# Conditioning units turned feature-major on VectorE, sums folded, a root spread by one product, and a 128-row spatial product for the samples

## The chip, the cores and the metric

The kernel runs on one core of a Trainium2 chip. The core has five engines with a queue each: TensorE (PE in the profile; its weight loads are PEld), VectorE (DVE), ScalarE (ACT), GpSimd (POOL) and SyncE (SP, which here issues nearly all transfers). Matrix products write to PSUM, a small memory of eight banks of 128 rows by 512 fp32 numbers; everything else lies in SBUF, 128 rows ("partitions") wide. The metric is the device time of one execution in microseconds, taken as the median of several runs. Less is better.

## What is computed

One step of a one-layer decoder for 256 prompt tokens and 8 samples of 4 tokens each: 288 tokens of 2048 features, all in fp32. Nine conditioning vectors (one of the prompt, eight of the samples) give six modulation vectors of 2048 features each.

```python
def _rms(x, gain):
    y = xf * lax.rsqrt(jnp.mean(xf * xf, axis=-1, keepdims=True) + EPS)
    return (y * gain.astype(jnp.float32)).astype(x.dtype)
...
    mod = (jax.nn.silu(c) @ w_ada + b_ada).reshape(n, N_MOD, 1, D_MODEL)
    sh_m, sc_m, gt_m, sh_f, sc_f, gt_f = [mod[:, i] for i in range(N_MOD)]

    h = _rms(x, g_mix) * (1 + sc_m) + sh_m
    proj = h @ w_in
    ...
    z = c_gate * hc
    ...
    ya = b_gate * conv

    u = jax.nn.gelu(u)
    v = _rms(jax.nn.gelu(v), g_v)
    vg = v.reshape(n, s // chunk, chunk, SG_GROUPS, SG_HEAD)
    w_causal = jnp.tril(w_sg[:, :chunk, :chunk])
    sp = jnp.einsum('gts,bnsgc->bntgc', w_causal, vg) + b_sg[:, :chunk].T[None, None, :, :, None]
    yb = u * sp.reshape(n, s, SG_DIM)

    merged = jax.nn.sigmoid(ga) * (ya @ w_pa) + jax.nn.sigmoid(gb) * (yb @ w_pb)
    x = x + gt_m * (merged @ w_out)

    h2 = _rms(x, g_ffn) * (1 + sc_f) + sh_f
    gate, up = jnp.split(h2 @ w_ffn_in, 2, axis=-1)
    x = x + gt_f * ((jax.nn.silu(gate) * up) @ w_ffn_out)
```

The outputs are the normalised `x` of both groups, the last rows of the convolution's input, and the normalised `v` rows.

## The kernel before

**Layout.** Activations are feature-major: a tile holds 128 features in its rows and the 288 tokens in its columns (256 of the prompt, then 32 of the samples). The weights stream from HBM in blocks of 1 MB or less into seven `raw` buffers. ACT rounds a segment of up to four 128x128 tiles to fp32r (`hi`, L444) and DVE makes the rest of it (`lo`, L450); there are four buffers of each. The activations are split in the same way (`split`, L274). One weight tile times one activation tile is a *triple* of three products (`triple`, L217 to L226): hi by hi, hi by lo, lo by hi.

**Order.** PE's order is that of the program throughout. Until the step `free`, the order of ACT, DVE and SP is the program's too; after it a planner orders them by its own estimate of which instruction is ready. POOL is always the planner's. The list `steps` holds blocks of weights (`Blk.run`), conditioning blocks (`Ada.run`) and small steps (`Do`). Small work on PE between triples goes through `later(f, gap)`: `drain`, called after each triple, runs the first entry of the list `pending` when `gap` triples have passed since the entry before it.

**Conditioning units.** The 96 blocks of 128 modulation features come in eight units (`ADA_UNITS`, L36). A unit of the kind `ks == 1` (aE, a2, a3, a4, a5) covers 16 feature blocks. For each of the 16 blocks of the contraction, four products with 32 columns of conditioning vectors (nine used) as weights and 512 columns of `w_ada` as the moving side run side by side on the four column quarters of the array, and leave a condition-major result in the bank `ada`: quarter j, rows 32j to 32j+8, holds feature blocks 4j to 4j+3 of the unit. `Ada.tail` (L387) copies it to SBUF on ACT (L390); three triples later four fp32 products with a selection matrix `sel` as the moving side (L400) make it feature-major, and four DVE adds (L404) put it into `mod` with the bias `b_ada`. The units aA, aC and aD (`ks == 2`) add two halves on the way, with `selk`.

**Norms.** `SquareSum` keeps a sum of squares in `acc` and the last square apart in `last`. `token_rstd` (L168) makes the sums over features on PE: three products with a column of ones for `acc`, and three for `last` into the same PSUM columns (`sums`, `square_sum` at L185); each product covers 128 tokens, at offsets 0, 128 and 160. `roots` (L194) scales them on DVE, and POOL raises them to the power -1/2 (L199). `token_rstd` serves the norm of `v` (`v_stats`) and the second norm (`rstd2`). The first norm (`sums1`, from the step `root`) has one set of sums, and the last one (`finish`) calls `sums` itself. `rstd_bcast` (L203) spreads the roots over 128 rows for norm 1 (`norm1`), norm 2 (`norm2`) and the end, with three fp32 products (L208): a root column, repeated, as weights by an identity, 128, 128 and 32 tokens wide; the last of them uses 32 rows of the array.

**Spatial gating.** `v_transpose` turns `v` token-major (L761) and scales it by the root and `g_v` (L763). For the samples (`tb == 2`) only rows 96 to 127 are scaled, which are the 32 sample tokens. `sg_load` loads and masks the spatial weights. `spatial(g)` (L795) makes three fp32 products for each of eight groups: two chunks of the prompt (L801, L802; 128 rows) and the samples (L803; 32 rows, 32 columns wide).

Of the kernel before, what the change touches and what calls it, by code (L numbers as in the profile page):

```python
# [29 lines left out]
GC = 0.044715  # L30
EPS = 1e-6

C_BADA, C_GMIX, C_SEL, C_SELK, C_ID, C1_END = np.cumsum([0, 96, 16, 36, 18, 128]).tolist()
C_GFFN, C_GFIN, C_WCONV, C_STATE, C_MASK, C_MASKS, C2_END = np.cumsum([0, 16, 16, 24, 128, 128, 32]).tolist()

ADA_UNITS = [  # L36
# [52 lines left out]
def _body(tc, nc, d, pc, pw, pslot, ptmp, pps):  # L89
    ids = [0]  # L90

    def nm(s):
        ids[0] += 1
        return f"{s}_{ids[0]}"
# [4 lines left out]
    def slot(dt=F32, shape=(P, T)):  # L99
        return pslot.tile(list(shape), dt, tag="s", name=nm("s"), padded_shape=[P, TU])  # L100

    def tmp(n=T):
        return ptmp.tile([P, n], F32, tag="t", name=nm("t"), padded_shape=[P, TU])
# [4 lines left out]
    def psmisc():  # L108
        return pps.tile([P, 512], F32, tag="misc", name=nm("px"), bufs=3)
# [15 lines left out]
    ident = cp1[:, C_ID : C_ID + 128]  # L125
    mask = cp[:, C_MASK : C_MASK + 128]
    masks = cp[:, C_MASKS : C_MASKS + 32]
    sel = cp1[:, C_SEL : C_SEL + 36]
    selk = cp1[:, C_SELK : C_SELK + 18]

    x = const("x", [P, 16, T])
# [35 lines left out]

    def token_rstd(ss, n, half=False, gaps=None):  # L168
        got = {}
        steps = [lambda: sums(got, ss, True), lambda: sums(got, ss, False), lambda: roots(got, n, half)]  # L170
        for f, gap in zip(steps, gaps or (0, 0, 0)):
            if gaps:
                later(f, gap)
            else:
                f()
        return got

    def sums(got, ss, first):
        if first:
            got["ps"] = psmisc()  # L180
        square_sum(got["ps"], ss.acc if first else ss.last, first, not first)
# [12 lines left out]
    def roots(got, n, half):  # L194
        ps = got["ps"]
        r = got["r"] = ptmp.tile([P, 3], F32, tag="r", name=nm("r"), bufs=2)
        e = ptmp.tile([P, 3], F32, tag="e", name=nm("e"), bufs=2)
        V.tensor_scalar(e, ps[:, 0:3], 1.0 / n, EPS, ALU.mult, ALU.add)
        G.tensor_tensor(r, e, mhalf[:, 0:3], ALU.pow)  # L199
        if half:  # L200
            V.tensor_scalar(r, r, 0.5, None, ALU.mult)

    def rstd_bcast(got):  # L203
        r = got["r"]
        ps = psmisc()
        for tb in range(3):
            a = 0 if tb < 2 else 96
            PE.matmul(  # L208
                ps[:, TB[tb] + a : TB[tb] + 128],
                r[a:, tb : tb + 1].to_broadcast([P - a, P]),  # L210
                ident[a:, a:],
                start=True,
                stop=True,
            )
        return ps[:, :T]
# [34 lines left out]
    def later(f, gap=0):  # L250
        if not pending:
            since[0] = 0
        pending.append((f, gap))
# [90 lines left out]
    class Ada(Step):  # L344
# [41 lines left out]

        def tail(self, gap=3, scaled=None, copied=None):  # L387
            w, ks, acc = self.nq * 128, self.ks, Ada.cur[self.name]
            ev = ptmp.tile([P, 512], F32, tag="ev", name=nm("ev"), bufs=1)
            A.copy(ev[:, :w], acc[:, :w])  # L390
            if copied:
                warm(2)
                copied()

            def rest():
                ps = psmisc()
                sl, ng = (sel, 4) if ks == 1 else (selk, 2)
                c = ng * NC
                for q in range(self.nq):
                    PE.matmul(ps[:, c * q : c * q + c], ev[:, 128 * q : 128 * q + 128], sl, start=True, stop=True)  # L400
                pv = ps[:, : c * self.nq].rearrange("p (q j i) -> p q j i", j=ng, i=NC)
                for j in range(ng):
                    f, nq = self.fb[j * ks], self.nq
                    V.tensor_tensor(  # L404
                        mod[:, f : f + nq, :],
                        pv[:, :, j, :],
                        bada[:, f : f + nq].unsqueeze(2).to_broadcast([P, nq, NC]),
                        ALU.add,
                    )
                    if scaled and j == 0:  # L410
                        scaled()

            if gap:
                later(rest, gap)
            else:
                rest()

    class Blk(Step):
        def __init__(self, name, idx, rhs, sink):
# [323 lines left out]
            SY.dma_start(d["o_z"], zout)  # L743

    def v_stats():
        S["rv"] = token_rstd(S["accv"], 4096, True, (1, 1, 0))
        S["gv"] = []
        for i in range(4):
            t = slot(shape=(P, 256))
            SY.dma_start(t, d["gv"][:, 256 * i : 256 * i + 256])  # L750
            S["gv"].append(t)

    def v_transpose():
        def one(i, tb):
            def f():
                rv = S["rv"]["r"]
                o = 96 if tb == 2 else 0
                ps = psmisc()
                for q in range(2):
                    a = part[32 + 2 * i + q]  # L760
                    PE.transpose(ps[:, 128 * q : 128 * q + 128], a[:, TB[tb] : TB[tb] + 128], ident)  # L761
                t = slot(shape=(P, 256))
                V.scalar_tensor_tensor(  # L763
                    t[o:], ps[o:, :256], rv[o:, tb : tb + 1], S["gv"][i][o:], ALU.mult, ALU.mult
                )
                vn[tb, i] = t
                if tb == 1:
                    SY.dma_start(d["o_vp"][:, 256 * i : 256 * i + 256], t)
                if tb == 2:
                    SY.dma_start(d["o_vs"][:, 256 * i : 256 * i + 256], t[96:])  # L770
                    for q in range(2):
                        part.pop(32 + 2 * i + q)

            return f

        for i in range(4):
            for tb in range(3):
                later(one(i, tb), 2)

    def sg_load():  # L780
        for i in range(4):
            t = slot(shape=(P, 256))
            SY.dma_start(t, d["wsg"][:, 256 * i : 256 * i + 256])
            tv = t.rearrange("p (g t) -> p g t", g=2)
            G.tensor_tensor(tv, tv, mask.unsqueeze(1).to_broadcast([P, 2, P]), ALU.mult)
            b = slot(shape=(P, 256))
            SY.dma_start(b, d["bsg"][:, 256 * i : 256 * i + 256])
            wsg[i] = (tv, b.rearrange("p (g t) -> p g t", g=2))
        t = slot(shape=(P, 256))[96:]
        SY.dma_start(t, d["wsgs"])  # L790
        tv = t.rearrange("p (g t) -> p g t", g=8)
        G.tensor_tensor(tv, tv, masks[96:].unsqueeze(1).to_broadcast([32, 8, 32]), ALU.mult)
        wsg["s"] = tv

    def spatial(g):  # L795
        def f():
            i, q = g // 2, g % 2
            sl = slice(128 * q, 128 * q + 128)
            w, b = wsg[i]
            ps = psmisc()  # L800
            PE.matmul(ps[:, 0:128], vn[0, i][:, sl], w[:, q, :], start=True, stop=True)  # L801
            PE.matmul(ps[:, 128:256], vn[1, i][:, sl], w[:, q, :], start=True, stop=True)  # L802
            PE.matmul(ps[:, 256:288], vn[2, i][96:, sl], wsg["s"][:, g, :], start=True, stop=True)  # L803
            t = tmp()
            V.tensor_tensor(
                t[:, :TP].rearrange("p (n t) -> p n t", n=2),
                ps[:, :TP].rearrange("p (n t) -> p n t", n=2),
                b[:, q, :].unsqueeze(1).to_broadcast([P, 2, P]),
                ALU.add,
            )  # L810
            V.tensor_tensor(
                sam(t[:, TP:]), sam(ps[:, TP:T]), b[:, q, :NS].unsqueeze(1).to_broadcast([P, NB, NS]), ALU.add
            )
            V.scalar_tensor_tensor(t, t, 0.5, u2[g], ALU.mult, ALU.mult)
            yb[g] = split(t)
            part.pop(24 + g)
            if q:
                wsg.pop(i)
                for tb in range(3):
                    vn.pop((tb, i))  # L820

        return Do(f)
# [35 lines left out]
    h2, xg = {}, {}  # L858

    def rstd2():  # L860
        S["r2"] = token_rstd(S["acc2"], D, gaps=(6, 3, 0))

    def norm2():
        ps = rstd_bcast(S["r2"])
# [3 lines left out]
    def mk_h2(k0, k1):  # L868
        def f():
            modulate(range(k0, k1), lambda k: normed(k, S["rb2"]), gm2, 48, h2)  # L870

        return Do(f)
# [77 lines left out]

    def root():
        later(sums1, 16)
        later(norm1, 7)

    plan = {2: [Do(root, None)], 5: aC[:4], 7: aC[4:] + [mk_h1(2, 5)]}
    steps += at(wA, plan)
# [31 lines left out]

    fk = [KBlk("fk", i, xg.__getitem__, sink_fk) for i in range(4)]
    nxt = ffin(1)  # L990
    steps += [fk[0], Do(norm2, 6), mk_h2(0, 6), fk[1], mk_h2(6, 11), fk[2], mk_h2(11, 16), fk[3]]
    steps += at(ffin(0) + nxt[:2], {2: a5[:4], 6: a5[4:8], 10: a5[8:12], 14: a5[12:]})
    for q in range(3):
        steps += ffout(q) + nxt[2:]
# [61 lines left out]
def _feat(v):  # L1056
    return np.ascontiguousarray(v.reshape(-1, P).T)
# [100 lines left out]
```

## Time and profile before

| what | value |
|---|---|
| median of three runs | 1649.07 us |
| lowest, highest | 1649.05, 1649.55 us |
| the profiled execution, its own time | 1649.16 us |
| its span, first to last instruction | 1647.4 us |
| mean granted clock of TensorE | 0.998 |
| moved by transfers | 357.60 MB, mean 217 GB/s |
| busy share of ACT, POOL | 45%, 1% |

The profile page gives the busy time of each engine, the busy share in 40 slices, the transfer queues, the chain of work that ended last (followed back from the last instruction), and the costliest groups of instructions. A group's line has: source line, engine, operation, result <- operands, shape, count | busy us in total, mean ns of one | us for which the engine was idle just ahead of them, and what ended most of that. A line of the timeline has: start in us, duration, engine, source line, operation, operands, shape, count where neighbours are merged, and in brackets idle time ahead of it. An fp32 product (unlike an fp32r one) leaves two records in the trace. The ends of products are modelled, their starts are recorded.

### The profile page before, as it was taken

What the parts mean: (1) busy time and instruction counts of PE and PEld (TensorE: products, weight loads), DVE (VectorE), ACT (ScalarE), POOL (GpSimd) and SP (SyncE); (2) the same over time, 40 slices, a digit from 0 to 9 for tenths busy, and PEclk for the clock granted to TensorE, in tenths of its full rate; (3) what the DMA queues carried; (4) which work ended last, traced back from release to release, by engine and by line L of the source; (5) the groups of instructions that cost most, each with busy time, mean ns of one, the idle gap of its engine ahead of it and who ended that gap; (6) DMA issues with size and microseconds to landing.
All of it is one profiled execution on the core that took longest, in us unless ns stands there. A gap on an engine that the chain in (4) does not pass through costs nothing.

```text
span 1647.4 us, 31135 instructions
## 1 busy us (share of the span) xinstructions
PE 1632.9 (99%) x12420; PEld 1556.7 (94%) x12420; DVE 1008.3 (61%) x2165; ACT 741.3 (45%) x1364; POOL 20.8 (1%) x66
## 2 busy tenths in 40 slices
PE   9999999999999999999999999999999999999997
PEld 6889899998998999999998999999999999999997
DVE  5567787877754557666844455555555555555565
ACT  4543344643444334456744444444444444444463
POOL 0000000000000000002000000000000000000000
PEclk9999999999999999999999999999999999999999
DMA  9777775667786667754586546443465434644341
GB/s 363 301 285 286 299 259 200 261 256 278 283 317 260 260 228 290 276 170 163 174 316 253 200 165 225 157 176 108 165 214 173 160 131 153 215 167 164 115 159 58
DMA packets 59426, 357.60 MB, mean 217 GB/s; under 512 B 6640, under 2 KB 9616, under 8 KB 28560
## 3 DMA queue, kind: packets, MB, share of 16 engines
q1 hardware_dynamic: 58992, 355.38, 59.2%
q8 instruction: 97, 1.59, 0.4%
q14 instruction: 49, 0.40, 0.1%
q10 hardware_dynamic: 288, 0.22, 0.1%
HBM read 352.49 MB, written 3.09 MB: 216 GB/s over the span
## 4 chain that ended last, share of the span: by engine, by line
PE 97%; DVE 1%; DMA 1%; ACT 0%; issue 0%; SPq 0%; DVEq 0%
PE pm L219 30%; PE pm L220 30%; PE pm L221 30%; PE ada L375 5%; DMA raw<-in_aA 1%; PE px L400 0%; DVE lo L450 0%; DVE x L921 0%; PE px L185 0%; PE pm L528 0%; DVE s L679 0%; PE px L801 0%; PE px L803 0%; PE px L761 0%; SPq L357 0%
## 5 line engine op out<-in xcount | busy, mean ns | idle before, releaser
L219 PE MATMUL pm<-s,hi 128*128 128x288 f32 (+1 forms) x3760 | 1112.2, 296 | 1.2 <-DVE s L679 0.9
L220 PE MATMUL pm<-s,hi 128*128 128x288 f32 (+1 forms) x3760 | 1110.2, 295 | 1.1 <-DVE s L595 0.7
L221 PE MATMUL pm<-s,lo 128*128 128x288 f32 (+1 forms) x3760 | 1109.5, 295 | 0.2 <-DVE lo L642 0.2
L450 DVE TENSOR_TENSOR lo<-raw,hi 128x512 fp32r<-128x512 f32 (+1 forms) x959 | 654.1, 682 | 496.4 <-ACT hi L444 476.8
L444 ACT CAST hi<-raw 128x512 fp32r<-128x512 f32 (+1 forms) x960 | 587.9, 613 | 797.4 <-PE pm L220 780.5
L219 PEld LDWEIGHTS pm<-s,hi 128*128 128x128 f32 x3760 | 707.2, 188 | 21.3 <-issue 15.9
L220 PEld LDWEIGHTS pm<-s,hi 128*128 128x128 f32 x3760 | 706.5, 188 | 2.1 <-DVE s L595 0.9
L221 PEld LDWEIGHTS pm<-s,lo 128*128 128x128 f32 x3760 | 706.6, 188 | 0.4 <-DVE lo L642 0.4
L375 PE MATMUL ada<-raw,cs 128*32 128x512 f32 (+2 forms) x832 | 89.0, 563 | 1.6 <-DMA raw<-in_aA 1.4
L375 PEld LDWEIGHTS ada<-raw,cs 128*32 128x32 f32 x832 | 23.8, 109 | 48.7 <-issue 43.2
L708 DVE TENSOR_TENSOR s<-pm,s 128x288 f32<-128x288 f32 x72 | 32.8, 456 | 14.8 <-PE pm L221 14.7
L319 DVE SCALAR_TENSOR_TENSOR x<-pm,mod,x 128x256 f32<-128x256 f32 x80 | 38.0, 475 | 2.7 <-PE pm L221 2.7
L276 ACT CAST s<-t 128x288 fp32r<-128x288 f32 (+1 forms) x76 | 32.6, 433 | 14.3 <-DVE t L740 7.1
L278 DVE TENSOR_TENSOR s<-t,s 128x288 fp32r<-128x288 f32 (+1 forms) x76 | 34.6, 459 | 6.9 <-ACT s L276 6.9
L700 DVE TENSOR_TENSOR s<-pm,s 128x288 f32<-128x288 f32 x56 | 25.2, 453 | 7.8 <-PE pm L221 7.8
L886 DVE SCALAR_TENSOR_TENSOR t<-t,pm 128x288 f32<-128x288 f32 x42 | 19.1, 454 | 16.5 <-PE pm L221 16.5
L325 DVE TENSOR_TENSOR t<-pm,mod 128x32 f32<-128x32 f32 x80 | 15.3, 192 | 19.2 <-PE pm L221 19.2
L677 ACT COPY s<-pm 128x298 f32<-128x298 f32 (+1 forms) x42 | 17.0, 404 | 18.4 <-PE pm L221 18.2
L160 ACT ACTIVATE t<-x 128x288 f32<-128x288 f32 (+2 forms) x31 | 13.5, 437 | 20.5 <-DVE x L328 17.3
L685 DVE SCALAR_TENSOR_TENSOR s<-pm,s 128x256 f32<-128x256 f32 x40 | 19.2, 481 | 5.0 <-PE pm L221 5.0
L165 DVE TENSOR_TENSOR acc<-acc,t 128x288 f32<-128x288 f32 x34 | 15.5, 455 | 8.2 <-ACT t L160 8.2
L404 DVE TENSOR_TENSOR mod<-px,cp 128x36 f32<-128x36 f32 (+2 forms) x26 | 3.5, 185 | 27.4 <-PE px L400 27.4
(126 smaller groups left out, 472.7 us busy)
## 6 DMA issues: line engine op xcount, KB each, us to landing
raw<-in_fi SPq DMA_DIRECT2D x84, 1024.0 KB, 4.8
raw<-in_a SPq DMA_DIRECT2D x64, 1024.0 KB, 9.7
raw<-in_f SPq DMA_DIRECT2D x64, 704.0 KB, 4.1
raw<-in_wD SPq DMA_DIRECT2D x36, 1024.0 KB, 5.0
raw<-in_wC SPq DMA_DIRECT2D x24, 768.0 KB, 5.2
raw<-in_aE SPq DMA_DIRECT2D x16, 1024.0 KB, 9.9
raw<-in_wo SPq DMA_DIRECT2D x16, 1024.0 KB, 5.0
raw<-in_pa SPq DMA_DIRECT2D x8, 1024.0 KB, 4.9
```

Of the source, the lines that this page charges most:

```text
L219: PE.matmul(out, wh, ah, start=first, stop=False)
L220: PE.matmul(out, wh, al, start=False, stop=False)
L221: lh = PE.matmul(out, wl, ah, start=False, stop=last)
L276: A.copy(hi, a)
L278: V.tensor_tensor(lo, a, hi.bitcast(F32), ALU.subtract)
L319: V.scalar_tensor_tensor(x[:, m, :TP], ps[:, :TP], mod[:, gt0 + m, 0:1], x[:, m, :TP], ALU.mult, ALU.add)
L375: PE.matmul(acc[32 * j : 32 * j + 32, :w], cs[:, kt, :], self.raw[:, o : o + w], start=(kt < ks), stop=(kt >= 16 - ks), tile_position=(0, ...
L444: A.copy(hi, self.raw[:, s * 128 : e * 128])
L450: sub()
L685: V.scalar_tensor_tensor(t[:, :TP], ps[:, :TP], t[:, T : T + 1], t[:, :TP], ALU.add, ALU.add)
L700: return V.tensor_tensor(part[m], ps[:, :T], part[m], ALU.add)
L708: V.tensor_tensor(a, ps[:, :T], a, ALU.add)
```

## The change

- Units with `ks == 1`: the products with `sel`, the copy on ACT and the four adds go. `turned`, three triples after the unit's end, transposes the bank `ada` on DVE in blocks of 32x32, straight from PSUM, and adds the bias in one instruction of 16 feature blocks, or in two of eight where the unit's features are not in a row (aE). For this the host lays out the unit's 2048 columns so that quarter j holds features 32j to 32j+31 of each of the 16 feature blocks. `sel` leaves the first pack of constants.
- `token_rstd`: one DVE add puts `last` into `acc` and one set of sums follows. The gaps become (2, 0) from (1, 1, 0) for `v`, and (9, 0) from (6, 3, 0) for norm 2.
- Norms 1 and 2: DVE makes a `diagonal` tile of 128x288 with each token's root at its row, four or five triples after the sums, and one fp32 product of a matrix of ones by this tile spreads the roots. The gap from the sums to the product is 5 + 3 triples at norm 1 (7 before), and 4 + 3 at norm 2 (6 before). The end keeps the three products.
- Samples' spatial product: all 128 rows of the token-major tile are scaled, the weight tile gets zeros in its first 96 rows (POOL), and the product uses 128 rows.

```diff
     def token_rstd(ss, n, half=False, gaps=None):
         got = {}
-        steps = [lambda: sums(got, ss, True), lambda: sums(got, ss, False), lambda: roots(got, n, half)]
+        V.tensor_tensor(ss.acc, ss.acc, ss.last, ALU.add)
+
+        def fold():
+            got["ps"] = psmisc()
+            square_sum(got["ps"], ss.acc, True, True)
+
+        steps = [fold, lambda: roots(got, n, half)]
         for f, gap in zip(steps, gaps or (0, 0, 0)):
...
+    def diagonal(got):
+        r = got["r"]
+        g = got["diag"] = tmp()
+        V.tensor_tensor(
+            g[:, :TP].rearrange("p (b t) -> p b t", b=2),
+            ident.unsqueeze(1).to_broadcast([P, 2, P]),
+            r[:, 0:2].unsqueeze(2).to_broadcast([P, 2, P]),
+            ALU.mult,
+        )
+        V.tensor_scalar(g[:, TP:], ident[:, 96:], r[:, 2:3], None, ALU.mult)
+
     def rstd_bcast(got):
         r = got["r"]
         ps = psmisc()
+        if "diag" in got:
+            PE.matmul(ps[:, :T], ones, got["diag"], start=True, stop=True)
+            return ps[:, :T]
         for tb in range(3):
...
         def tail(self, gap=3, scaled=None, copied=None):
             w, ks, acc = self.nq * 128, self.ks, Ada.cur[self.name]
+            if ks == 1:
+                return later(lambda: self.turned(acc), gap)
...
+        def turned(self, acc):
+            ev = ptmp.tile([P, 512], F32, tag="ev", name=nm("ev"), bufs=1)
+            V.transpose(ev, acc)
+            tv = ev.rearrange("p (b i) -> p b i", i=32)[:, :, :NC]
+            runs = [(self.fb[0], 16)] if self.fb[3] == self.fb[0] + 12 else [(self.fb[0], 8), (self.fb[2], 8)]
+            o = 0
+            for f, n in runs:
+                V.tensor_tensor(
+                    mod[:, f : f + n, :],
+                    tv[:, o : o + n],
+                    bada[:, f : f + n].unsqueeze(2).to_broadcast([P, n, NC]),
+                    ALU.add,
+                )
+                o += n
...
     def v_stats():
-        S["rv"] = token_rstd(S["accv"], 4096, True, (1, 1, 0))
+        S["rv"] = token_rstd(S["accv"], 4096, True, (2, 0))
...
-                o = 96 if tb == 2 else 0
...
                 V.scalar_tensor_tensor(
-                    t[o:], ps[o:, :256], rv[o:, tb : tb + 1], S["gv"][i][o:], ALU.mult, ALU.mult
+                    t, ps[:, :256], rv[:, tb : tb + 1], S["gv"][i], ALU.mult, ALU.mult
                 )
...
-        t = slot(shape=(P, 256))[96:]
-        SY.dma_start(t, d["wsgs"])
+        t = slot(shape=(P, 256))
+        G.memset(t[:96], 0.0)
+        SY.dma_start(t[96:], d["wsgs"])
...
-            PE.matmul(ps[:, 256:288], vn[2, i][96:, sl], wsg["s"][:, g, :], start=True, stop=True)
+            PE.matmul(ps[:, 256:288], vn[2, i][:, sl], wsg["s"][:, g, :], start=True, stop=True)
...
     def rstd2():
-        S["r2"] = token_rstd(S["acc2"], D, gaps=(6, 3, 0))
+        S["r2"] = token_rstd(S["acc2"], D, gaps=(9, 0))
+        later(lambda: diagonal(S["r2"]), 4)
...
     def root():
         later(sums1, 16)
-        later(norm1, 7)
+        later(lambda: diagonal(S["r1"]), 5)
+        later(norm1, 3)
...
-    steps += [fk[0], Do(norm2, 6), mk_h2(0, 6), fk[1], mk_h2(6, 11), fk[2], mk_h2(11, 16), fk[3]]
+    steps += [fk[0], Do(norm2, 3), mk_h2(0, 6), fk[1], mk_h2(6, 11), fk[2], mk_h2(11, 16), fk[3]]
...
-            s = np.stack(cols, 2)
+            s = np.stack(cols, 2).reshape(16, P, 16, 4, 32).swapaxes(2, 3)
```

More of the change, by code (lines that the diff above doesn't have):

```diff
@@ L31 @@
 EPS = 1e-6
-C_BADA, C_GMIX, C_SEL, C_SELK, C_ID, C1_END = np.cumsum([0, 96, 16, 36, 18, 128]).tolist()
+C_BADA, C_GMIX, C_SELK, C_ID, C1_END = np.cumsum([0, 96, 16, 18, 128]).tolist()
 C_GFFN, C_GFIN, C_WCONV, C_STATE, C_MASK, C_MASKS, C2_END = np.cumsum([0, 16, 16, 24, 128, 128, 32]).tolist()
@@ L127, in _body @@
     masks = cp[:, C_MASKS : C_MASKS + 32]
-    sel = cp1[:, C_SEL : C_SEL + 36]
     selk = cp1[:, C_SELK : C_SELK + 18]
@@ L396, in rest @@
                 ps = psmisc()
-                sl, ng = (sel, 4) if ks == 1 else (selk, 2)
-                c = ng * NC
+                ng, c = 2, 2 * NC
                 for q in range(self.nq):
-                    PE.matmul(ps[:, c * q : c * q + c], ev[:, 128 * q : 128 * q + 128], sl, start=True, stop=True)
+                    PE.matmul(ps[:, c * q : c * q + c], ev[:, 128 * q : 128 * q + 128], selk, start=True, stop=True)
                 pv = ps[:, : c * self.nq].rearrange("p (q j i) -> p q j i", j=ng, i=NC)
@@ L788, in sg_load @@
             wsg[i] = (tv, b.rearrange("p (g t) -> p g t", g=2))
-        t = slot(shape=(P, 256))[96:]
-        SY.dma_start(t, d["wsgs"])
+        t = slot(shape=(P, 256))
+        G.memset(t[:96], 0.0)
+        SY.dma_start(t[96:], d["wsgs"])
         tv = t.rearrange("p (g t) -> p g t", g=8)
-        G.tensor_tensor(tv, tv, masks[96:].unsqueeze(1).to_broadcast([32, 8, 32]), ALU.mult)
+        G.tensor_tensor(tv[96:], tv[96:], masks[96:].unsqueeze(1).to_broadcast([32, 8, 32]), ALU.mult)
         wsg["s"] = tv
@@ L1076 @@
     masks[96:] = (r[:, None] // NS == r[None, :] // NS) & (r[:, None] <= r[None, :])
-    sel = np.zeros((P, 36), np.float32)
     selk = np.zeros((P, 18), np.float32)
@@ L1080 @@
         for i in range(NC):
-            sel[32 * j + i, NC * j + i] = 1
             selk[32 * j + i, NC * (j // 2) + i] = 1
-    arr["cpack1"] = np.ascontiguousarray(np.concatenate([_feat(a["b_ada"][0]), _feat(a["g_mix"][0]), sel, selk, np.eye(P, dtype=np.float32)], 1))
+    arr["cpack1"] = np.ascontiguousarray(np.concatenate([_feat(a["b_ada"][0]), _feat(a["g_mix"][0]), selk, np.eye(P, dtype=np.float32)], 1))
     arr["cpack2"] = np.ascontiguousarray(
```

## The prediction, made before the changed kernel ran

> **What bounds the kernel now.** I read the page first: busy times and the chain that ended last.
>
> ```profile
> span 1647.4 us, 31135 instructions
> ...
> PE 1632.9 (99%) x12420; PEld 1556.7 (94%) x12420; DVE 1008.3 (61%) x2165; ACT 741.3 (45%) x1364; POOL 20.8 (1%) x66
> ...
> PE 97%; DVE 1%; DMA 1%; ACT 0%; issue 0%; SPq 0%; DVEq 0%
> ```
>
> TensorE (PE) is busy nearly throughout and makes up 97% of the chain. A busy PE can still be a PE that runs slowly or waits between products, so I next read the groups of instructions, with shapes kept apart, for the three products of a triple (L219 to L221).
>
> ```profile
> L219 PE MATMUL pm<-s,hi 128*128 128x288 f32 x3632 | 1073.0, 295 | 0.9 <-DVE s L679 0.9
> L220 PE MATMUL pm<-s,hi 128*128 128x288 f32 x3632 | 1071.8, 295 | 1.0 <-DVE s L595 0.7 <-DVE s L302 0.3
> L221 PE MATMUL pm<-s,lo 128*128 128x288 f32 x3632 | 1071.0, 295 | 0.0
> ```
>
> The last field is the idle time ahead of the group: 1.9 us for 10,896 products. PE waits for almost nobody. What counts then is the start-to-start step in the timeline of PE (start, duration, instruction), not the 295 ns, since products overlap. Here is the place where one conditioning unit is turned:
>
> ```profile
> 908.83 0.30 PE L220 MATMUL pm<-s,hi 128*128 128x288 f32 x1
> 908.96 0.29 PE L221 MATMUL pm<-s,lo 128*128 128x288 f32 x1
> 909.09 0.97 PE L400 MATMUL px<-cp,ev 128*128 128x36 f32 x8
> 909.90 0.38 PE L219 MATMUL pm<-s,hi 128*128 128x288 f32 x1
> 910.11 0.29 PE L220 MATMUL pm<-s,hi 128*128 128x288 f32 x1
> ```
>
> A product follows the last after 0.13 us, so a triple costs 0.40 us. The method for everything below: an insertion costs the time from its own start to the start of the second product behind it (the first one behind it starts slowly), less the 0.13 us that these two would need anyway. Since PE is the chain, each insertion removed takes its cost from the end, unless PE then waits for something.
>
> **Part 1: five conditioning units turned on VectorE (DVE).** The insertion above costs 910.11 - 909.09 - 0.13 = 0.89 us. It is four fp32 products, and each is recorded twice.
>
> ```profile
> L400 PE MATMUL px<-cp,ev 128*128 128x36 f32 x40 | 4.9, 268 | 0.0
> L404 DVE TENSOR_TENSOR mod<-px,cp 128x36 f32<-128x36 f32 x20 | 2.6, 188 | 16.7 <-PE px L400 16.7
> L390 ACT COPY ev<-ada 128x512 f32<-128x512 f32 x5 | 2.9, 587 | 11.1 <-PE ada L375 11.1
> L450 DVE TENSOR_TENSOR lo<-raw,hi 128x512 fp32r<-128x512 f32 x895 | 618.3, 691 | 448.4 <-ACT hi L444 428.7 <-DMA raw<-in_wD 4.7 <-issue 0.2
> L847 DVE SCALAR_TENSOR_TENSOR gm<-mod,cp 128x144 f32<-128x144 f32 x1 | 0.3, 311 | 0.0
> ```
>
> 40 records are 5 units, all of which lose their four products: 5 x 0.89 = **4.45 us**. ACT loses five copies of 0.59 us. DVE loses four adds of 0.19 us a unit and gains a block transpose of 128x512 and one add of 144 elements (aE: two of 72). The transpose has no row. Its lower bound is the 0.19 us add, its upper the nearest full pass over 512 columns doubled, 1.4 us; I take 0.69 us. In place of 0.75 us DVE then works some 1.0 us, and DVE is idle for 4.20 us ahead of the adds of the last unit. Nothing on PE waits for them soon: the values are used blocks later. I cost it at nothing; without that cover it would be 0.3 us a unit. The Trainium skill (VectorE: DVE Perf Modes, "The three transpose paths") has 311 ns for a 128x128 bf16 block transpose; four of them give an estimate of 1.2 us, by which the sum stays as it is. No run here shows it yet.
>
> **Part 2: sums folded.**
>
> ```profile
> 320.02 0.72 PE L185 MATMUL px<-ones,acc 128*128 128x1 f32 x6
> 320.61 0.38 PE L219 MATMUL pm<-s,hi 128*128 128x288 f32 x1
> 320.83 0.30 PE L220 MATMUL pm<-s,hi 128*128 128x288 f32 x1
> ```
>
> Three products against a column of ones cost 320.83 - 320.02 - 0.13 = 0.68 us. v_stats and rstd2 each drop one of two such insertions: 2 x 0.68 = **1.35 us**. The price is one DVE add of 128x288 each (0.45 us) ahead of the products; what it may delay is a rival below. The sums of norm 1 and the end keep their form.
>
> **Part 3: root spread by one product.** norm1 and norm2 use three fp32 products (two of 128 columns, one of 32 rows); the end keeps them.
>
> ```profile
> 783.00 0.94 PE L208 MATMUL px<-cp,r 128*128 128x128 f32 x6
> 783.87 0.41 PE L219 MATMUL px<-s,hi 128*128 128x298 f32 x1
> 784.11 0.30 PE L220 MATMUL px<-s,hi 128*128 128x298 f32 x1
> ```
>
> ```profile
> L375 PE MATMUL ada<-raw,cs 128*32 128x512 f32 x640 | 72.8, 595 | 0.0
> ```
>
> Now: 784.11 - 783.00 - 0.14 = 0.97 us. An fp32 product 288 wide has no row. L375 (its row stands in the groups) runs four records side by side, one on each quarter of the columns of the array: 160 groups in 72.8 us, 0.455 us per 512 columns, so 0.26 us per 288; two records 0.51, plus 0.22 from the first to the second product behind, less 0.13, gives 0.60. Saved 0.37, twice: **0.75 us**. Bounds: nothing, if the wide product costs as much as the three, to 1.3, if it costs no more than one 128 wide (two steps of 0.11 and 0.22, less 0.13: 0.31). I stay near the row for 512 columns, since it alone has wide records. The diagonal adds two DVE instructions (0.45 and 0.2 us) behind the power on POOL (0.85 us, row below). For rstd2, r comes about 1.1 us after the sums, the diagonal 0.65 us later, and PE gets there seven triples after the sums, 2.9 us: 1.1 us of room, enough for one L450 of 0.69 us between. At norm1 the gap is eight triples. While the diagonal waits for r, the splits of weights and the evictions queue behind it on DVE and PE behind those; a wait is the 0.85 us of the power at most, less than one split buffer of four triples (1.6 us) lasts PE.
>
> **Part 4: samples' spatial product over 128 rows.**
>
> ```profile
> 560.56 0.38 PE L801 MATMUL px<-s,s 128*128 128x128 f32 x2
> 560.78 0.39 PE L802 MATMUL px<-s,s 128*128 128x128 f32 x2
> 561.09 0.40 PE L803 MATMUL px<-s,s 32*128 32x32 f32 x2
> 561.43 0.49 PE L801 MATMUL px<-s,s 128*128 128x128 f32 x2
> ...
> 562.64 0.29 PE L220 MATMUL pm<-s,hi 128*128 128x288 f32 x1
> ```
>
> From L801 to L802 the step is 0.22 us, but into the 32-row product it is 0.31 and out of it 0.34. A pair of groups costs 562.64 - 560.56 - 0.13 = 1.95 us for 12 records. With 128 rows throughout, I extend the eight records of L400 (0.89 us) by four steps of 0.11 and 0.08 for the wider first record: 1.42. Saved 0.53, four pairs: **2.1 us**. Bounds: nothing to 2.6. The Trainium skill speaks against it: "K=32 single mm = same time as K=128" (TensorE: Matmul & The Clock Gate, "Why this matters for your kernels"); by that this part would bring 0 and the whole 6.35. Another of its pages has "Mode switching requires drain" (TensorEngine Tiling (Array Packing), "Key Properties"), and the steps of 0.31 and 0.34 beside 0.22 agree with this one. The other work is small: the multiplication on DVE is as wide per row as before, and the zero fill on POOL, busy 1% of the span, runs long ahead. In the transfers only 36 columns (18 KB) of the first constants go, off ACT's queue, which PE does not wait for; the samples' small weights stay at their place in SP's queue and land in the last 32 rows as before.
>
> **The sum.** 4.45 + 1.35 + 0.75 + 2.1 = 8.65 us. One thing I take off. Behind norm2, DVE makes the second input without a break, and PE is just behind it (timelines of POOL, DVE and PE):
>
> ```profile
> 780.59 0.85 POOL L199 TENSOR_TENSOR r<-e,mhalf 128x3 f32<-128x3 f32 x1 [3.46 <-DVE e L198]
> ```
>
> ```profile
> 809.50 0.45 DVE L893 TENSOR_TENSOR s<-pm,rb 128x288 f32<-128x288 f32 x1
> ```
>
> ```profile
> 810.13 0.33 PE L219 MATMUL pm<-s,hi 128*128 128x288 f32 x1
> ```
>
> L893 frees a PSUM buffer at 809.95 and PE needs one at 810.13: 0.18 us of room. PE comes there 0.68 + 0.37 = 1.05 us earlier; the spread root comes earlier by that less one triple (the gaps add to 16 triples in place of 15), 0.65 us. The difference of 0.40 eats the 0.18 and leaves a stall of 0.2 us. So 8.45 us. The profiled execution took 1649.16 us (span 1647.4), 0.09 above the median of the three runs, 1649.07: 1649.07 - 8.45 = **1640.6 us**.
>
> **Rivals.**
> 1. New waits for DVE. The fold's add stands behind everything of the sink before it. In v_stats PE reaches the products at 320.02 + 0.40 = 320.42.
>
> ```profile
> 314.71 0.45 DVE L165 TENSOR_TENSOR acc<-acc,t 128x288 f32<-128x288 f32 x1
> 315.08 0.30 DVE L333 TENSOR_SCALAR t<-t 128x288 f32<-128x288 f32 x1
> ...
> 319.83 0.46 DVE L708 TENSOR_TENSOR s<-pm,s 128x288 f32<-128x288 f32 x1
> 320.41 0.69 DVE L450 TENSOR_TENSOR lo<-raw,hi 128x512 fp32r<-128x512 f32 x1
> ```
>
> In program order it would start after L708, at 320.3, or after L450, at 321.1, and PE would wait 0.3 to 1.1 us; the same at rstd2, and up to 0.6 more behind norm2. Against it: L165 runs ahead of L333, which the program has before it, so the order lets a ready add pass. About 2 us given back: 1642.6. Chance 0.17.
> 2. The change does not do what it says in part 4: 128 rows cost what 32 do, by a drain that belongs to any fp32 product. For it only the rule above; against it the steps. 1640.6 + 2.1 = 1642.7. Chance 0.10.
> 3. More goes than the products: the stalls in the first three rows of PE (1.9 us idle, with restarts some 2.3 us) dissolve when DVE loses adds and ACT copies. Nearly 2 us more, 1638.7. Chance 0.06: four of five units end behind those stalls.
> 4. **Slower**: the transpose is slow, a row at a time. Weights are split four tiles of four ahead, 16 triples or 6.4 us; a transpose of X us holds up the splits behind it on DVE and stalls PE by X - 6.4, five times. The gain is gone at X = 8.1 us; at 9.5 us the kernel takes 1640.6 + 15.5 = 1656.1. Against it: that is 14 times the pass of 0.69 us. Chance 0.04.
>
> **How the numbers follow.** Forecast 0.63, rivals 0.17, 0.10, 0.06, 0.04. Low end: the full 8.65 with 0.5 more from part 4 and half of rival 3, 10.3 us, so 1638.8. High end: rivals 1 and 2 together, 8.45 - 2.1 - 2 = 4.35, so 1644.7. About 0.2%, 3.3 us, is what a measurement of this kernel can tell from no change: faster is below 1645.8. All cases but the last lie there; some of rivals 1 and 2 may lie deeper than worked out, so faster 0.91, same 0.05, slower 0.04.
>
> **What would show it.** In the changed profile: the 40 records of L400 with 36 columns gone; PE steps without the 0.89 us at five places; one group of sums at v_stats and at rstd2 with no DVE releaser in front of it; the spread by three products left only at the end; steps of 0.11 through the spatial groups; DVE busy up by 2 to 4 us; the transpose at 0.5 to 1.4 us. Wrong would be: PE idle ahead of the sums or of the one product, idle behind the second input grown by over 0.5 us, a step above 0.3 into the wider sample product, or idle time on PE, released by L450, after a transpose.

## The result

| | median | lowest, highest | runs |
|---|---|---|---|
| before | 1649.15 us | 1649.05, 1649.55 | 6 |
| after | 1643.2 us | 1643.07, 1643.26 | 6 |

The ratio is 0.9963, with a 95% interval of 0.9950 to 0.9976. The change gained 5.95 us; the forecast was 8.45 us. The profiled execution of the changed kernel took 1643.07 us, 6.09 less than that of before, and its page begins and carries the chain so:

```profile
span 1641.3 us, 31007 instructions
...
PE 1625.7 (99%) x12360; PEld 1550.4 (94%) x12360; DVE 1011.1 (62%) x2162; ACT 738.7 (45%) x1359; POOL 21.7 (1%) x67
...
PE 96%; DVE 1%; DMA 1%; ACT 1%; issue 0%; DVEq 0%; ACTq 0%; SPq 0%
```

PE still is the chain. Its busy time fell by 7.2 us but the span by 6.1: PE now has new gaps. The groups by form show the new work on DVE (four of the new adds, L445, take 1.2 us more), and in the last field a wait that the kernel before did not have, 0.8 us ahead of the new product:

```profile
L440 DVE STREAM_TRANSPOSE ev<-ada 128x512 f32<-128x512 f32 x5 | 3.6, 717 | 7.6 <-PE ada L394 7.6
L223 PE MATMUL px<-t,ones 128*128 128x288 f32 x4 | 1.5, 458 | 0.8 <-DVE t L217 0.8
L211 DVE TENSOR_TENSOR t<-cp,r 128x256 f32<-128x256 f32 x2 | 0.8, 422 | 1.0 <-POOL r L204 1.0
```

In the changed file the three products of a triple are L238, L239 and L240, the split that makes `lo` is L485, the one that makes `hi` is L479, and an eviction by DVE is L714. To find where the time went, the starts of the 3,776 triples were compared, triple by triple; a difference that grows or shrinks at a place is what that place costs.

| place | forecast | measured |
|---|---|---|
| five units | -4.45 | -4.45 (0.89 each) |
| two sums | -1.35 | -1.34 (0.67 each) |
| four pairs of spatial groups | -2.1 | -2.44 (0.61 each) |
| spread at norm 1 | -0.37 | +0.35 |
| spread at norm 2 | -0.38 | -0.05 |
| stall behind norm 2 | +0.2 | none |
| a new stall at 51.65 us | - | +0.71 |
| a changed step between products | - | +1.4 |
| start of the first triples | - | -0.3 |
| sum | -8.45 | -6.1 |

The last row but one is taken as scatter of the start: in the kernels below the first triple starts between 0.54 us earlier and 0.10 us later than in the kernel before, and in `late8`, whose program up to there is that of the kernel before, 0.34 us earlier. Some of the errors cancel: part 3 fell short by 1.05 us and the new stall and step cost 2.1, against which part 4 gave 0.34 more, the stall behind norm 2 did not come (0.2) and the start gave 0.3. The three losses follow.

**Norm 1.** The timeline of PE where the roots are spread:

```profile
43.74 0.30 PE L240 MATMUL pm<-s,lo 128*128 128x298 f32 x1
44.63 0.75 PE L223 MATMUL px<-t,ones 128*128 128x288 f32 x2 [0.60 <-DVE t L217]
45.01 0.52 PE L238 MATMUL pm<-s,hi 128*128 128x298 f32 x1
45.36 0.30 PE L239 MATMUL pm<-s,hi 128*128 128x298 f32 x1
```

The new product could start at 43.88, 0.14 us behind L240, and starts at 44.63: 0.75 us of waiting. The timelines of POOL and DVE say for what:

```profile
40.94 1.40 POOL L204 TENSOR_TENSOR r<-e,mhalf 128x3 f32<-128x3 f32 x1 [23.43 <-DVE e L203]
```

```profile
43.40 0.69 DVE L485 TENSOR_TENSOR lo<-raw,hi 128x512 fp32r<-128x512 f32 x1 [1.31 <-ACT hi L479]
44.01 0.42 DVE L211 TENSOR_TENSOR t<-cp,r 128x256 f32<-128x256 f32 x1
44.34 0.23 DVE L217 TENSOR_SCALAR t<-cp,r 128x32 f32<-128x32 f32 x1
```

The power is done at 42.34, and DVE stands idle for 1.31 us until 43.40. But the split comes ahead of the diagonal in DVE's order, and the split waits for ACT. So the diagonal, whose input is there, starts 1.67 us after the power's end.

**The stall.** Seven microseconds on, PE stands still where the kernel before did not:

```profile
51.65 0.30 PE L240 MATMUL pm<-s,lo 128*128 128x298 f32 x1
52.40 0.40 PE L238 MATMUL pm<-s,hi 128*128 128x298 f32 x1 [0.45 <-DVE s L714]
```

It waits for a bank that an eviction has to empty. The timeline of DVE shows that this eviction stands behind a split that itself waits for ACT:

```profile
51.27 0.69 DVE L485 TENSOR_TENSOR lo<-raw,hi 128x512 fp32r<-128x512 f32 x1 [0.70 <-ACT hi L479]
51.88 0.46 DVE L714 COPY s<-pm 128x298 f32<-128x298 f32 x1
```

In the kernel before, the same split starts at 50.73 without a wait and the eviction at 51.33. On ACT, three instructions that make the first normalised input (one L617, two L624) now stand between this split's rounding (L479 at 50.62) and the one before it; in the kernel before only one does (L589), and the rounding starts at 50.07.

**The step.** The starts of two products of the input projection, 168 products apart in the same work, in the timelines of PE of before and of after:

```profile
340.60 0.29 PE L219 MATMUL pm<-s,hi 128*128 128x288 f32 x1
...
362.70 0.29 PE L219 MATMUL pm<-s,hi 128*128 128x288 f32 x1
```

```profile
340.29 0.29 PE L238 MATMUL pm<-s,hi 128*128 128x288 f32 x1
...
362.55 0.29 PE L238 MATMUL pm<-s,hi 128*128 128x288 f32 x1
```

22.10 us became 22.26: a product follows the last after 132.5 ns in place of 131.5. The durations of single products (0.29) do not show it, nor is any idle time marked. Over the whole stretch from 300 to 560 us, some 1,700 products, the mean step is 132.5 ns in place of 131.8, which makes 1.2 us; smaller shares of both signs elsewhere bring it to 1.4.

### The profile page after: what moved, and what is told of

Read it like the earlier page. It is cut to its first block, busy times and chain, and to the rows that moved or that the text cites. A ratio compares the mean times of both kernels' runs of the same rounds, so it can differ in the third digit from the quotient of the medians.

```text
span 1641.3 us, 31007 instructions
## 1 busy us (share of the span) xinstructions
PE 1625.7 (99%) x12360; PEld 1550.4 (94%) x12360; DVE 1011.1 (62%) x2162; ACT 738.7 (45%) x1359; POOL 21.7 (1%) x67
## 4 chain that ended last, share of the span: by engine, by line
PE 96%; DVE 1%; DMA 1%; ACT 1%; issue 0%; DVEq 0%; ACTq 0%; SPq 0%
PE pm L238 30%; PE pm L239 30%; PE pm L240 30%; PE ada L394 5%; DMA raw<-in_wA 1%; DMA raw<-in_aA 1%; DVE lo L485 0%; ACT hi L479 0%; DVE x L957 0%; DMA ct<-in_c 0%; DVE s L714 0%; PE px L190 0%; PE px L795 0%; PE px L836 0%; DVE s L302 0%
## 5 line engine op out<-in xcount | busy, mean ns | idle before, releaser
L238 PE MATMUL pm<-s,hi 128*128 128x288 f32 (+1 forms) x3760 | 1112.9, 296 | 1.6 <-DVE s L714 1.3
L239 PE MATMUL pm<-s,hi 128*128 128x288 f32 (+1 forms) x3760 | 1110.3, 295 | 1.1 <-DVE s L630 0.7
L240 PE MATMUL pm<-s,lo 128*128 128x288 f32 (+1 forms) x3760 | 1109.7, 295 | 0.2 <-DVE lo L677 0.2
L485 DVE TENSOR_TENSOR lo<-raw,hi 128x512 fp32r<-128x512 f32 (+1 forms) x959 | 654.2, 682 | 497.7 <-ACT hi L479 483.7
L479 ACT CAST hi<-raw 128x512 fp32r<-128x512 f32 (+1 forms) x960 | 588.0, 613 | 801.1 <-PE pm L239 787.1
L238 PEld LDWEIGHTS pm<-s,hi 128*128 128x128 f32 x3760 | 707.1, 188 | 21.9 <-issue 15.9
L239 PEld LDWEIGHTS pm<-s,hi 128*128 128x128 f32 x3760 | 706.8, 188 | 2.2 <-DVE s L630 0.9
L240 PEld LDWEIGHTS pm<-s,lo 128*128 128x128 f32 x3760 | 706.4, 188 | 0.4 <-DVE lo L677 0.4
L743 DVE TENSOR_TENSOR s<-pm,s 128x288 f32<-128x288 f32 x72 | 32.9, 457 | 15.9 <-PE pm L240 15.8
L204 POOL TENSOR_TENSOR r<-e,mhalf 128x3 f32<-128x3 f32 x4 | 4.2, 1040 | 1159.5 <-DVE e L203 1159.5
```

Of the source, the lines that this page charges most:

```text
L238: PE.matmul(out, wh, ah, start=first, stop=False)
L239: PE.matmul(out, wh, al, start=False, stop=False)
L240: lh = PE.matmul(out, wl, ah, start=False, stop=last)
L479: A.copy(hi, self.raw[:, s * 128 : e * 128])
L485: sub()
L743: V.tensor_tensor(a, ps[:, :T], a, ALU.add)
```

## Experiments

Two theories stood for the stall and the step. By one, they come from a place in the order: the gap from the sums of norm 1 to its spread is 5 + 3 = 8 triples in place of 7, which shifts all that follows on the engines. By the other, they come with the new work (the diagonal, the transposes on DVE).

### The spread of norm 1 one triple earlier

`early_43` makes the gap 7 triples again and puts the diagonal, one triple earlier, ahead of the split. (It also changes the gap given to `norm2`, which turned out to have no effect: `norm2` stands at the end of the block `fk[0]`, 16 triples behind its start, in every kernel here. So the half of theory Q on norm 2 is not tried by these two kernels, and the wait there stayed in both.) `early_44` takes the diagonal earlier in the same way but keeps 8 triples.

```diff
-        later(lambda: diagonal(S["r1"]), 5)
+        later(lambda: diagonal(S["r1"]), 4)
         later(norm1, 3)
...
-Do(norm2, 3)
+Do(norm2, 4)
```

> The changed kernel with the diagonal one triple earlier at norm 1 (gaps 4 and 3, 7 triples in all as before the change) and the spreading product one triple later at norm 2 (4 and 4). Theory Q: the two waits of PE for the diagonal (0.76 and 0.33 us) come from a split of weights that stands ahead of it on DVE; both vanish. Theory P: the stall of 0.71 us near 52 us and the slower step in the input projection from 300 to 560 us (132.5 ns for 131.8, some 1.2 us in all) come from norm 1's one triple more, which moves the small jobs behind it by an eviction and their results to other buffers; both vanish too, so 1643.2 - 0.76 - 0.33 - 0.71 - 1.2 = 1640.2 us, with a step of 131.8 ns. Rival R: the step has another cause in the change (turned units, folded sums, wider products): step 132.5, 1641.4 us.

```diff
-        later(lambda: diagonal(S["r1"]), 5)
-        later(norm1, 3)
+        later(lambda: diagonal(S["r1"]), 4)
+        later(norm1, 4)
```

> As the run before, but norm 1's gaps are 4 and 4, 8 triples in all, as in the changed kernel. Q: no wait for the diagonal. P: the stall near 52 us and the step of 132.5 ns stay, 1643.2 - 0.76 - 0.33 = 1642.1 us. Rival S: both are echoes of PE's wait at norm 1 and go with it, 1640.2 us.

`early_43` took 1640.45 us (1640.12 to 1640.8, four runs; ratio to before 0.9947, interval 0.9932 to 0.9961); `early_44` took 1642.3 us (1642.09 to 1643.34, five runs; 0.9957, interval 0.9943 to 0.9971). The timelines of DVE and of PE in `early_43`:

```profile
42.48 0.43 DVE L211 TENSOR_TENSOR t<-cp,r 128x256 f32<-128x256 f32 x1 [0.28 <-POOL r L204]
42.83 0.23 DVE L217 TENSOR_SCALAR t<-cp,r 128x32 f32<-128x32 f32 x1
43.52 0.69 DVE L485 TENSOR_TENSOR lo<-raw,hi 128x512 fp32r<-128x512 f32 x1 [0.46 <-ACT hi L479]
```

```profile
43.45 0.30 PE L240 MATMUL pm<-s,lo 128*128 128x298 f32 x1
43.59 0.65 PE L223 MATMUL px<-t,ones 128*128 128x288 f32 x2
43.86 0.51 PE L238 MATMUL pm<-s,hi 128*128 128x298 f32 x1
44.21 0.30 PE L239 MATMUL pm<-s,hi 128*128 128x298 f32 x1
...
338.33 0.29 PE L238 MATMUL pm<-s,hi 128*128 128x288 f32 x1
...
360.43 0.29 PE L238 MATMUL pm<-s,hi 128*128 128x288 f32 x1
```

The diagonal now runs as soon as the power is done, the split behind it, and PE does not wait. The wide product by itself costs 44.21 - 43.59 - 0.14 = 0.48 us, less than the 0.60 estimated. Its saving against the three products (0.98 at norm 1) is 0.50 where it is not waited for. The stall is gone, and the 168 products take 22.10 us again, 131.5 ns each. In `early_44` the wait at norm 1 is gone too, but the stall (0.7 us) and the step (132.5 ns) are there. So the wait at norm 1 belongs to the place of the diagonal, and stall and step to the eighth triple, with the same work on DVE in both kernels.

### The spread by three products, with the rest of the change

`three` keeps parts 1, 2 and 4 and undoes part 3, at the old gaps.

```diff
-        later(lambda: diagonal(S["r2"]), 4)
...
-        later(lambda: diagonal(S["r1"]), 5)
-        later(norm1, 3)
+        later(norm1, 7)
...
-Do(norm2, 3)
+Do(norm2, 6)
```

> The changed kernel with part 3 undone: three products spread the root at norms 1 and 2, gaps of 7 and 6, no diagonal. Each spread costs 0.98 us again, in place of 1.35 and 0.92: 0.3 us less. P: the stall near 52 us goes and the step returns to 131.8 ns: 1643.2 - 0.3 - 0.7 - 1.2 = 1641.0 us. R: the step stays at 132.5, 1642.2 us. If the spread by one product were a gain as forecast, this would be slower than the changed kernel: 1644 us.

1641.07 us (1640.94 to 1641.58, four runs; 0.9951, interval 0.9936 to 0.9966): 2.1 us less than the whole change. Part 3, as it was placed, lost time: some 0.3 us by the spreads themselves, and the rest by the eighth triple that came with it. The mean step in the input projection is 131.8 ns as in the kernel before, and there is no stall.

### The eighth triple alone

`late8` is the kernel before with nothing changed but the gap of norm 1.

```diff
-        later(norm1, 7)
+        later(norm1, 8)
```

> The kernel before the change with one number changed: norm 1's spread 8 triples behind the sums in place of 7. No diagonal, no stall for it. P: a stall of some 0.7 us near 52 us and a step of 132.5 ns from 300 to 560 us, 1649.15 + 0.7 + 1.2 = 1651.0 us. S and R: no change, 1649.15 us.

1651.42 us (1651.19 to 1652.49, ten runs; 1.0013, interval 1.0004 to 1.0023), 2.2 us slower than before. Its timeline of PE shows the stall at the same place:

```profile
51.58 0.30 PE L221 MATMUL pm<-s,lo 128*128 128x298 f32 x1
52.14 0.41 PE L219 MATMUL pm<-s,hi 128*128 128x298 f32 x1 [0.26 <-DVE s L679]
```

The comparison of starts gives 0.54 us for the stall and 1.6 us for the step, which is 132.5 ns in the input projection. None of the four parts is in this kernel, so none is needed for either loss. In the program, the eighth triple puts the spread behind an eviction that it stood ahead of. The first input is made in small jobs, one after each eviction (`evicted`); they then come one eviction later, and since they take their buffers at that point, by the program the splits of the activations lie at other places of SBUF from there on. The altered order itself ends early: in the traces of `late8` and of the kernel before, PE, DVE, ACT and POOL carry out the same instructions, by operation, names and shapes, in the same order from 52 us on. What can differ between 300 and 560 us is the time at which they run, and the places. The time does not do it: `three` and `early_44` both start the work that the kernel before does at 300 us some 0.8 us earlier, and their 168 products take 22.10 and 22.26 us.

### The places alone

Whether the places alone change the step is told by `slots_1`: it is `early_43` with one buffer of the common pool taken, one column of it cleared and nothing read from it, so that buffers taken later lie elsewhere. The order of instructions on PE, DVE, ACT and SP is that of `early_43`. `slots_5` takes five.

```diff
+    G.memset(slot()[:, 0:1], 0.0)
```

> The kernel early_43 with one slot asked for and cleared on GpSimd ahead of the others; it holds nothing of use. Each engine but GpSimd has the same instructions in the same order, only the place in SBUF of some slots differs (of the eight input pairs of the input projection, the pairs 4, 5 and 3 take other slots). Theory P2: the step of the products hangs on where the operands lie, so the step from 300 to 560 us moves off 131.8 ns by over 0.2 ns, in a direction that I can't tell. Rival T: what slowed the step was the later time of the small jobs, and the step stays at 131.8 ns and the time at 1640.4 us.

> As slots_1 with five slots asked for and cleared: another placement, the same instructions in the same order. P2: again another step than 131.8 ns in the input projection; T: 131.8 ns and 1640.4 us.

`slots_1` took 1641.28 us (1641.21 to 1641.42, four runs; 0.9952, interval 0.9937 to 0.9967), `slots_5` 1641.62 us (1641.49 to 1641.73, four runs; 0.9954, interval 0.9937 to 0.9970). The timeline of PE in `slots_1`, the same 168 products:

```profile
338.25 0.29 PE L238 MATMUL pm<-s,hi 128*128 128x288 f32 x1
...
360.56 0.29 PE L238 MATMUL pm<-s,hi 128*128 128x288 f32 x1
```

22.31 us, 132.8 ns a product against 131.5, with the same instructions in the same order. `slots_5` has that step too. So where the buffers of the pool lie in SBUF sets the step, here by up to 1%. The activations that the products read are among the buffers that moved; tiles that DVE and ACT read and write meanwhile moved too, and the runs do not tell the two apart. In other stages `slots_1` is the faster one (131.8 against 132.6 ns from 138 to 180 us), which is why its end differs from that of `early_43` by only 0.8 us. Which addresses go well together was not found.

### Part 1 alone, and part 4 undone

`turned_only` is the kernel before with the units turned on DVE:

```diff
+            if ks == 1:
+                return later(lambda: self.turned(acc), gap)
...
+            V.transpose(ev, acc)
...
-            s = np.stack(cols, 2)
+            s = np.stack(cols, 2).reshape(16, P, 16, 4, 32).swapaxes(2, 3)
```

> The kernel before with part 1 alone: the five units turned on DVE. Norm 1 keeps its 7 triples, so by P the placement is that of before and the step 131.8 ns; five insertions of 0.89 us go: 1649.2 - 4.45 = 1644.8 us. Rival R (the turned units slow the step): 1646.0 us. Rival: DVE's transposes of 0.72 us hold up splits, and PE idles behind them: over 1646 us.

1644.85 us (1644.46 to 1645.38, nine runs; 0.9974, interval 0.9964 to 0.9984): 4.46 us less than the 1649.31 of before beside it. The comparison of starts gives 4.45, five steps of 0.88 to 0.91.

`rows_32` is the changed kernel with the samples' spatial product over 32 rows again:

```diff
-                    t, ps[:, :256], rv[:, tb : tb + 1], S["gv"][i], ALU.mult, ALU.mult
+                    t[o:], ps[o:, :256], rv[o:, tb : tb + 1], S["gv"][i][o:], ALU.mult, ALU.mult
...
-            PE.matmul(ps[:, 256:288], vn[2, i][:, sl], wsg["s"][:, g, :], start=True, stop=True)
+            PE.matmul(ps[:, 256:288], vn[2, i][96:, sl], wsg["s"][96:, g, :], start=True, stop=True)
```

> The changed kernel with part 4 undone: the samples' spatial product over 32 rows again. By the steps of the two traces each of the four pairs of groups costs 0.6 us more: 1643.2 + 2.4 = 1645.6 us. Rival, the rule that 32 rows take as long as 128: 1643.2 us.

1645.6 us (1645.24 to 1645.91, ten runs; 0.9977, interval 0.9968 to 0.9987), 2.4 us more than the whole change; the comparison of starts gives four steps of 0.6. The timeline of PE in the changed kernel, one pair of groups, shows why part 4 brought more than forecast:

```profile
559.48 0.38 PE L836 MATMUL px<-s,s 128*128 128x128 f32 x2
559.70 0.39 PE L837 MATMUL px<-s,s 128*128 128x128 f32 x2
559.92 0.31 PE L838 MATMUL px<-s,s 128*128 128x32 f32 x2
560.06 0.47 PE L836 MATMUL px<-s,s 128*128 128x128 f32 x2
...
560.95 0.30 PE L239 MATMUL pm<-s,hi 128*128 128x288 f32 x1
```

The step into the samples' product fell from 0.31 to 0.22 us, and out of it from 0.34 to 0.14. The pair costs 560.95 - 559.48 - 0.13 = 1.34 us, against 1.95 before.

### The diagonal of norm 2

One wait was left in `early_43`. The timelines of DVE and PE of the changed kernel at norm 2 show its kind:

```profile
775.34 0.69 DVE L485 TENSOR_TENSOR lo<-raw,hi 128x512 fp32r<-128x512 f32 x1
775.94 0.16 DVE L203 TENSOR_SCALAR e<-px 128x3 f32<-128x3 f32 x1
777.07 0.42 DVE L211 TENSOR_TENSOR t<-cp,r 128x256 f32<-128x256 f32 x1 [0.96 <-POOL r L204]
777.41 0.68 DVE L485 TENSOR_TENSOR lo<-raw,hi 128x512 fp32r<-128x512 f32 x1
778.01 0.23 DVE L217 TENSOR_SCALAR t<-cp,r 128x32 f32<-128x32 f32 x1
```

```profile
778.30 0.75 PE L223 MATMUL px<-t,ones 128*128 128x288 f32 x2 [0.17 <-DVE t L217]
...
779.03 0.30 PE L239 MATMUL px<-s,hi 128*128 128x298 f32 x1
```

The scaling of the sums stands behind one split, the second half of the diagonal behind another. `fold_7` is `early_43` with the sums, and with them the diagonal, two triples earlier; the spread stays.

```diff
-        S["r2"] = token_rstd(S["acc2"], D, gaps=(9, 0))
+        S["r2"] = token_rstd(S["acc2"], D, gaps=(7, 0))
```

> early_43 with the sums of the second normalisation, and with them the diagonal, two triples (0.8 us) earlier; the spread stays where it is. In early_43 PE still waits about 0.33 us at the second spread for the diagonal. Theory N (the wait is the time of the power and of two splits between sums and diagonal, and a lead of 0.8 us covers it): the wait goes and the add of the two shares is ready in time: 1640.45 - 0.33 = 1640.1 us. Rival F (the add that folds the two shares follows the squares too late for sums that stand 0.8 us earlier): PE waits at the sums instead, 0.3 us or more, and the time stays at 1640.4 to 1640.7 us. The step of the products in the input projection should stay at 131.8 ns, since the places are those of early_43.

1639.77 us (1639.71 to 1641.25, four runs; ratio to before 0.9945, interval 0.9928 to 0.9963). Its timelines of DVE and PE:

```profile
771.25 0.16 DVE L203 TENSOR_SCALAR e<-px 128x3 f32<-128x3 f32 x1 [1.18 <-PE px L190]
...
772.52 0.42 DVE L211 TENSOR_TENSOR t<-cp,r 128x256 f32<-128x256 f32 x1 [0.74 <-POOL r L204]
...
774.45 0.23 DVE L217 TENSOR_SCALAR t<-cp,r 128x32 f32<-128x32 f32 x1
```

```profile
774.87 0.65 PE L223 MATMUL px<-t,ones 128*128 128x288 f32 x2
775.14 0.52 PE L238 MATMUL px<-s,hi 128*128 128x298 f32 x1
775.49 0.30 PE L239 MATMUL px<-s,hi 128*128 128x298 f32 x1
```

Two splits of weights and one of an activation still run between the halves, but PE no longer waits, neither here nor at the sums, whose add had ended 0.4 us ahead of them. The spread costs 775.49 - 774.87 - 0.14 = 0.48 us as at norm 1, where the changed kernel and `early_43` pay 0.92: 0.44 less, the 0.33 expected and 0.11 because the spread takes 0.62 us up to the second product behind it (774.87 to 775.49), where behind a wait it takes 0.73 (778.30 to 779.03). The medians differ by 0.7 us, but the runs of the two kernels overlap and the trace carries only the 0.44. This is the fastest kernel of the study, 3.4 us below the whole change and 9.46 below the 1649.23 of before beside it.

## Why the prediction was right and wrong

- **Range and sign** held: 1643.2 lies within 1638.8 to 1644.7. The likeliest time was 2.6 us too low. That the range reached so far up is in part luck: its upper end was rivals 1 and 2 together, and neither happened as told; what did cost time was not in the sum. One sign of being wrong that the prediction named did appear: PE idle ahead of the one product.
- **Part 1** was right to the hundredth, with the cover named: DVE's transpose took 0.72 us (0.69 taken), and no triple waited behind it. The rival of a slow transpose fell with that. By the Trainium skill (VectorE: DVE Perf Modes, "The three transpose paths") four bf16 transposes of 128x128 would make some 1.2 us, an estimate; the one fp32 transpose of 128x512 measured here took 0.72.
- **Part 2** was right, 0.67 a place against 0.68. The first rival, which had PE wait for the fold's add, did not happen. The timelines of DVE and PE in the changed kernel, at `v_stats`:

```profile
318.16 0.45 DVE L169 TENSOR_TENSOR acc<-acc,t 128x288 f32<-128x288 f32 x1
...
320.21 0.45 DVE L743 TENSOR_TENSOR s<-pm,s 128x288 f32<-128x288 f32 x1
```

```profile
320.75 0.72 PE L190 MATMUL px<-ones,acc 128*128 128x1 f32 x6
321.33 0.38 PE L238 MATMUL pm<-s,hi 128*128 128x288 f32 x1
321.55 0.29 PE L239 MATMUL pm<-s,hi 128*128 128x288 f32 x1
```

The add starts 2.6 us ahead of the sums and two us ahead of the last eviction L743; as argued against the rival, a ready add passes what the program has before it. The insertion is 321.55 - 320.75 - 0.13 = 0.67.

- **Part 3** is the step that failed, in the sentence "1.1 us of room, enough for one L450 of 0.69 us between. At norm1 the gap is eight triples." It counted the time from the root to PE and one split in between. The runs showed that it is the place in DVE's queue that decides. At norm 1 the diagonal stood behind a split that itself waited 1.31 us for ACT; at norm 2 two splits came between, not one. The power at norm 1 took 1.40 us, not the 0.85 read at norm 2, but it had ended 1.67 us before the diagonal began, so it is not what PE waited for. The rows of this power and of this split stood in the timelines of POOL and DVE of the kernel before; the prediction used only the row of norm 2:

```profile
41.22 1.40 POOL L199 TENSOR_TENSOR r<-e,mhalf 128x3 f32<-128x3 f32 x1 [23.36 <-DVE e L198]
```

```profile
43.69 0.69 DVE L450 TENSOR_TENSOR lo<-raw,hi 128x512 fp32r<-128x512 f32 x1 [1.31 <-ACT hi L444]
```

  In the prediction the queue was named, but only for what stands behind the diagonal, not for what it stands behind. Without waits the part is worth more than forecast: 0.50 and 0.49 us, since the wide product costs 0.48. As placed, it cost 0.30 us in place of saving 0.75.
- **The eighth triple** was costed at nothing, without a word. It is the largest loss: 0.71 us of stall and about 1.4 us by the step. `late8` shows both without the rest of the change, `early_43` shows the rest without them. No row of the profile before could give the size of the second, but that a step moved past an eviction shifts the jobs behind it could be read from the program.
- **Part 4** had the right mechanism, and the term was too small: 2.44 us against 2.1. A product 32 columns wide behind one 128 wide steps on after 0.14 us, where 0.22 had been allowed. By the rule "K=32 single mm = same time as K=128" of the Trainium skill (TensorE: Matmul & The Clock Gate, "Why this matters for your kernels") this part would have brought nothing; `rows_32` is 2.4 us slower, so here the rule gives the wrong time. It speaks of one product by itself, which no run here shows. "Mode switching requires drain" (TensorEngine Tiling (Array Packing), "Key Properties") agrees with the steps of 0.31 and 0.34 us, which only the 32-row form has.
- **The 0.2 us behind norm 2** did not show. The step failed at "the gaps add to 16 triples in place of 15": the gap given to `norm2` has no effect, and the spread stands where it stood before.
- **The first rival's time**, 1642.6, was near the result, but for another reason: DVE was waited for at the diagonals and at an eviction, not at the fold's add.

## What to carry to other kernels

An instruction added to an in-order queue is late by what stands ahead of it there, and that by what it waits for itself: read the row of the instruction ahead and its bracket, not only the time that the input takes. When a step is moved by even one unit of work, list the jobs that then change sides with it, since they shift evictions and the places that a pool hands out. When the parts of a change each measure as forecast but the sum does not, compare the starts of the repeated work one by one: a step that was longer by 1 ns in 131 showed here neither in the durations nor as idle time.

## What the runs showed of the hardware

- The step of the same 168 fp32r products (128x128 weights, 288 columns) in the same order was 131.5 ns in the kernel before and `early_43`, 132.5 in the changed kernel and 132.8 in `slots_1`, where only the places of buffers in SBUF differ from `early_43`. The granted clock was 0.998 in these four. Which buffers matter, and what in their addresses, stays open.
- An fp32 product 288 columns wide between fp32r products added 0.48 us, half of the 0.98 of two 128 wide and one over 32 rows.
- The power of 128x3 numbers on POOL at norm 1 took 1.40 us in eight of the eleven traces, the kernel before among them, and 0.85 or 0.86 in the other three (`slots_1`, `slots_5`, `fold_7`); at norm 2 it took 0.85 us before and after. What makes the difference stays open.
